# Grouped-query softmax weights scaled before their transposes, output kept feature-major

## The chip, the cores and the metric

The kernel runs on one core of one Trainium2 chip. The metric is device time in microseconds of one execution. Three timed runs of the kernel before gave a median of 2794.3 us (2793.43 to 2796.57). TensorE (PE) multiplies into the partial-sum memory PSUM, VectorE (DVE) and ScalarE (ACT) read PSUM and SBUF, GpSimd (POOL) reads SBUF, and SyncE (SP) issues the transfers.

## The reference

The whole model has two layers over 1024 tokens of width 1024. The change lies in the first layer, in the grouped-query attention, one of two head groups whose outputs go side by side into one output projection:

```python
def gqa_attention(q, k, v):
    scale = HEAD_DIM ** -0.5

    def block(qb):
        s = jnp.einsum('bqgrd,bkgd->bgrqk', qb, k).astype(jnp.float32) * scale
        pr = jax.nn.softmax(s, axis=-1).astype(v.dtype)
        return jnp.einsum('bgrqk,bkgd->bqgrd', pr, v)

    return from_blocks(lax.map(block, to_blocks(q)))
...
    a_o = rms_norm(diff_attention(a_q, a_k, a_v, lam), subln) * (1.0 - lam_init)
...
    b_o = gqa_attention(b_q, b_k, b_v)
    mix = jnp.concatenate([a_o.reshape(b, s, A_V), b_o.reshape(b, s, B_Q)], axis=-1)
    return mix @ w_out
```

There are eight query heads of 64 features and two key-value heads, so four query heads share one key-value head. After this mixer come a gated feed-forward with a convolution, a gated input embedding, a second layer with neighbourhood attention, and a final norm. All data is float32.

## The kernel before, in words

**Precision.** A float32 product is made of three fast ones: each operand is split into a high part (a copy to the type fp32r) and a low part (operand minus high part). A helper, `mm3` (lines 172 to 177), issues high by high, low by high and high by low. The high part is usually a copy on ACT, the low part a subtraction on DVE.

**Units and steps.** The function `even` computes the first mixer. It has six units: 0 to 3 are the four differential heads (A), 4 and 5 the two key-value groups of the grouped-query heads (B). A list `its` holds the steps (line 1087): eight blocks of 128 queries for each A unit, which makes steps 0 to 31, and eight blocks with four heads j = 0 to 3 for each B unit, which makes steps 32 to 95. Two B heads make a pair, an even step and the odd step after it.

**What one B step does.** `qk(n)` (line 955) computes the 128 x 1024 scores of a head into a PSUM tile S (two such tiles exist) by four matmuls, two with 128 rows (L969) and two with 64 (L974), and DVE takes the negated row maximum (L977). `exp(n)` (L986) has ACT write P = exp(S - max) to SBUF and the row sums to a small column. `combine(n)` (line 989) does, on odd steps alone, the reciprocal of both sums of a pair (L1001). `tr(n)` (line 1003) turns P on PE by eight 128 x 128 transposes (L1012) into two PSUM banks, and ACT copies the high part to `pt` (L1022); `tr2(n)` has DVE subtract for the low part (L1034). `pv(n)`, on odd steps alone, multiplies both heads of a pair by the values in sixteen matmuls of 256 columns (L1049). The stationary operand holds the high part of the values in its first 64 columns and the low part in the other 64, so output partitions 0 to 63 and 64 to 127 hold two shares of the same 64 features, and the columns are 2 x 128 queries. `tail_a(n)` adds the shares: ACT copies the upper half (L1066), DVE adds it to the lower (L1067). `tail_b(n)` turns the 64 x 256 sum back to queries by features with two PE transposes (L1078), and DVE multiplies by the reciprocals into a 256-wide tile `MS` (L1083). After four heads `place_b` hands two 128 x 128 halves of `MS` to `place` (line 1090), which transposes them again (L1095), because the output projection wants features on partitions, and splits them into H, its operand (ACT L1098, DVE L1099).

**Order.** The order is written out by hand: `step(n)` (line 1111) is a generator in two halves, and every engine runs its instructions in the order in which the program issues them. For a B step n the first half is: scores of n and their maximum; transposes of n-2 with ACT's copies; exponential of n; low parts of n-2. The second half is: `combine(n)`; on the steps where n-3 is odd, that is even n, `pv(n-3)`; `tail_b(n-4)`, which does something on odd n; `tail_a(n-3)`; and on every fourth step `place_b(n-5)`. The driver (lines 1180 to 1204) puts other work between the halves or behind them, by lists at the top of the file: a piece of the output projection's first half (`GEMM`: steps 57, 59, 61, 63, then 67, 70, 73 and so on to 100; twelve 512-column matmuls at L175 to L177 and a DVE addition at L258), the last input projection (`PROJ5`: 33, 35 and 37 among the B steps; 24 matmuls of 384 columns, then copies by ACT and DVE), transposes and splits of the next unit's queries and keys (`FIN4`: steps 28 to 32; `FIN5`: 49 to 59, odd; their DVE part, L922 or L942 to L945, comes between the halves of the step after), and the placing of the A heads (`PLACE`: 40 to 54, even; four transposes, and L1098 and L1099 of 512 columns). Weight tiles are split by `W.pump` (L164, L165) as room comes free. POOL's rotary embedding for the last unit runs in pieces in the first B steps.

**Buffers.** PSUM has four banks (`psb`) that are handed out in turn to transposes, values, tails, placing and projection; a new user waits until the one four places earlier is read out. SBUF tiles `os` come from a pool of seven, small columns from one of 24.

Of the kernel before, what the change touches and what calls it, by code (L numbers as in the profile page):

```python
# [11 lines left out]
F32 = mybir.dt.float32  # L12
F32R = mybir.dt.float32r
AF = mybir.ActivationFunctionType
ALU = mybir.AluOpType
# [10 lines left out]
P = 128  # L26
# [80 lines left out]
class Kern:  # L107
# [662 lines left out]
    def even(self, W, ready, load, after):  # L770
        nc, a = self.nc, self.a
# [25 lines left out]
        own = (slice(0, 64), slice(64, 128))  # L797
        bg = deque()

        def background(n):  # L800
            while bg and n > 0:
                bg.popleft()()
                n -= 1
# [149 lines left out]
        L, MS = {}, {}  # L953

        def qk(n):
            u, qt, j = its[n]
            A = u < 4
            if A and qt == 0:
                M[u] = self.u([P, NT, P], F32, "mix")
            qs, ks, kl = st[u]["q"], st[u]["k"], st[u]["kl"]  # L960
            e = L[n] = {"P": [], "nm": [], "S": []}
            e["s"] = self.col(2) if j % 2 == 0 else L[n - 1]["s"]
            bs = (0, 1) if A else (j,)
            qc = slice(qt * P, (qt + 1) * P)
            halves = (slice(0, 512), slice(512, 1024))
            for b in bs:
                ps = self.tS()
                for hk in halves:
                    nc.tensor.matmul(ps[:, hk], qs[b][:, qc], ks[b % 2][:, hk], start=True, stop=False)  # L969
                e["S"].append(ps)  # L970
            for hk in halves:
                for b, ps in zip(bs, e["S"]):
                    o = own[b % 2]
                    nc.tensor.matmul(ps[:, hk], qs[b][o, qc], kl[o, hk], start=False, stop=True)  # L974
            for ps in e["S"]:
                nm = self.col()
                nc.vector.tensor_reduce(nm, ps, axis=AX.X, op=ALU.max, negate=True)  # L977
                e["nm"].append(nm)

        def exp(n):  # L980
            u, qt, j = its[n]
            e = L[n]
            for b, (ps, nm) in enumerate(zip(e.pop("S"), e.pop("nm"))):
                p = self.u([P, S], F32, "P")
                c = b if u < 4 else j % 2
                nc.scalar.activation(p, ps, AF.Exp, bias=nm, accum_out=e["s"][:, c:c + 1])  # L986
                e["P"].append(p)

        def combine(n):
            u, qt, j = its[n]  # L990
            e = L[n]
            if u < 4:
                r = e["r"] = self.col(3)
                s0 = e["s"][:, 0:1]
                nc.vector.reciprocal(r[:, 0:2], e["s"])
                nc.vector.scalar_tensor_tensor(r[:, 2:3], s0, nlam, r[:, 1:2], op0=ALU.mult, op1=ALU.mult)
                nc.vector.scalar_tensor_tensor(e["P"][0], e["P"][1], r[:, 2:3], e["P"][0],
                                               op0=ALU.mult, op1=ALU.add)
            elif j % 2 == 1:
                r = e["r"] = self.col(2)  # L1000
                nc.vector.reciprocal(r, e["s"])  # L1001

        def tr(n):
            u, qt, j = its[n]
            e = L[n]
            w = e.pop("P")[0]
            e["T"] = []
            for h in range(2):
                ps = self.tb()
                for b in range(4):  # L1010
                    kt = 4 * h + b
                    nc.tensor.transpose(ps[:, b * P:(b + 1) * P], w[:, kt * P:(kt + 1) * P], self.ident)  # L1012
                e["T"].append(ps.rearrange("p (b c) -> p b c", b=4))
            if u < 4:
                e["pt"] = self.u([P, NT, P], F32, "pt")
            else:
                if j % 2 == 0:
                    e["pt"] = [[self.u([P, 4, 2, P], F32R, "pt") for _ in range(2)] for _ in range(2)]
                else:
                    e["pt"] = L[n - 1]["pt"]  # L1020
                for h in range(2):
                    nc.scalar.copy(e["pt"][h][0][:, :, j % 2], e["T"][h])  # L1022
# [13 lines left out]
        def pv(n):  # L1036
            u, qt, j = its[n]
            e = L[n]
            v = st[u]["v"]
            if u < 4:  # L1040
                o = e["o"] = self.tb()
                for kt in range(NT):
                    nc.tensor.matmul(o[:, :P], e["pt"][:, kt, :], v[:, kt, :], start=(kt == 0), stop=(kt == NT - 1))
                e.pop("pt")
            elif j % 2 == 1:
                o = e["o"] = self.tb()
                for kt in range(NT):
                    for x in range(2):
                        nc.tensor.matmul(o[:, :256], v[:, kt, :], e["pt"][kt // 4][x][:, kt % 4].rearrange("p a b -> p (a b)"),  # L1049
                                         start=(kt + x == 0), stop=(kt == NT - 1 and x == 1))  # L1050
                e.pop("pt")
                L[n - 1].pop("pt")

        def tail_a(n):
            u, qt, j = its[n]
            e = L[n]
            if u < 4:
                os = e["os"] = self.os()
                ss = self.col()
                xo = M[u][:, qt, :]  # L1060
                nc.scalar.activation(os[:, :P], e["o"][:, :P], AF.Copy, scale=e["r"][:, 0:1])
                nc.scalar.activation(xo, os[:, :P], AF.Square, accum_out=ss)
                e["rs"] = self.rstd(ss, 1.0 / P)
            elif j % 2 == 1:
                os = e["os"] = self.os()
                nc.scalar.copy(os[0:64], e["o"][64:128, :256])  # L1066
                nc.vector.tensor_add(os[0:64], e["o"][0:64, :256], os[0:64])  # L1067

        def tail_b(n):
            u, qt, j = its[n]  # L1070
            e = L[n]
            if u < 4:
                xo = M[u][:, qt, :]
                nc.vector.scalar_tensor_tensor(xo, e["os"][:, :P], e["rs"], gs, op0=ALU.mult, op1=ALU.mult)
            elif j % 2 == 1:
                ps = self.tb()
                for b in range(2):
                    nc.tensor.transpose(ps[:, b * 64:b * 64 + 64], e["os"][0:64, b * P:(b + 1) * P],  # L1078
                                        self.ident[0:64, 0:64])
                if j == 1:  # L1080
                    MS[u, qt] = self.os()
                xo = MS[u, qt][:, (j // 2) * P:(j // 2 + 1) * P].rearrange("p (h d) -> p h d", h=2)
                nc.vector.tensor_mul(xo, ps[:, :P].rearrange("p (h d) -> p h d", h=2),  # L1083
                                     e["r"][:, :, None].to_broadcast([P, 2, 64]))
            L.pop(n)

        its = [(u, qt, j) for u in range(6) for qt in range(NT) for j in range(1 if u < 4 else 4)]
        N = len(its)

        def place(src, k0, t):  # L1090

            ps = self.tb()
            n = len(src)
            for k, x in enumerate(src):
                nc.tensor.transpose(ps[:, k * P:(k + 1) * P], x, self.ident)  # L1095
            v = ps[:, :n * P].rearrange("p (k c) -> p k c", k=n)
            h, l = self.hT2(slice(k0, k0 + n), slice(t * P, (t + 1) * P))
            nc.scalar.copy(h, v)  # L1098
            nc.vector.tensor_sub(l, v, h.bitcast(F32))  # L1099
# [6 lines left out]
        def place_b(n):  # L1106
            u, qt, j = its[n]
            ms = MS.pop((u, qt))
            place([ms[:, :P], ms[:, P:]], 2 * u - 4, qt)

        def step(n):

            A = lambda m: 0 <= m < 32
            B = lambda m: 32 <= m < N
            if n < N:
                qk(n)
            if A(n - 2):
                pv(n - 2)
            if B(n - 2):
                tr(n - 2)  # L1120
            if n < N:
                exp(n)
            if B(n - 2):
                tr2(n - 2)
            if A(n - 2):
                tail_a(n - 2)
            if A(n - 4):
                tail_b(n - 4)
            yield
            if A(n - 1):  # L1130
                tr(n - 1)
                tr2(n - 1)
            if n < N:
                combine(n)
            if B(n - 3):
                pv(n - 3)
            if B(n - 4):
                tail_b(n - 4)
            if B(n - 3):
                tail_a(n - 3)  # L1140
            if B(n - 5) and its[n - 5][2] == 3:
                place_b(n - 5)
            background(4 if n < 32 else 2)
            yield
# [35 lines left out]
        for n in range(N + 6):  # L1180
# [4 lines left out]
            s = step(n)  # L1185
# [511 lines left out]
```

## Time and profile before

| | before |
|---|---|
| median of three runs | 2794.3 us |
| the profiled execution's own time | 2795.31 us |
| its span | 2793.3 us |
| granted TensorE clock, mean | 0.995 |
| ACT busy over the span | 1405.2 us (50%) |
| POOL busy over the span | 668.1 us (24%) |

The span is the time from the first to the last instruction; the execution's own time has 2 us more around it. Lines of the profile name an engine, a source line of the kernel, the operation and its tiles; "PEld" is the weight load that goes ahead of a matmul, and its start shows best when PE takes up the next piece of work. In a timeline a line gives the start, the duration, what ran and how often in a row; in square brackets stands the idle time ahead of it with what ended it. "Issue" means that nothing that the profile shows was waited for. The grouped-query steps run from about 375 to 661 us.

### The profile page before, as it was taken

How to read it: one execution, taken by the hardware profiler on the slowest of the kernel's cores; microseconds unless marked ns; L12 is line 12 of the kernel's file. 1: busy time of each engine (PE TensorE's matmuls, PEld its weight loads, DVE VectorE, ACT ScalarE, POOL GpSimd, SP SyncE). 2: the span in 40 equal slices, each digit the busy share in tenths (PEclk: the TensorE clock that was granted, in tenths of full speed). 3: DMA queues.
4: the chain of work that ended last, by engine and by line, in shares of the span. 5: the costliest groups of instructions: out<-in, count | busy, mean ns of one | idle time of the engine just before them, and what ended most of it. 6: DMA issues, size and time to landing. Idle time of an engine off the chain costs nothing. (4 is left out here: it accounts for less than half of the span.)

```text
span 2793.3 us, 37183 instructions
## 1 busy us (share of the span) xinstructions
PE 2734.1 (98%) x13776; PEld 2265.0 (81%) x13776; DVE 1920.2 (69%) x3004; ACT 1405.2 (50%) x2727; POOL 668.1 (24%) x756
## 2 busy tenths in 40 slices
PE   8999999999999999999999999999999999999998
PEld 8988877777788888888887878877878888888887
DVE  5677878775777777677635666666677777767753
ACT  4455567563444444534523666766344444453532
POOL 2222751000544444100101001000244444400000
PEclk9999999999999999999999999999999999999999
DMA  4000001101134333833211111124023343472411
GB/s 161 1 24 24 27 9 46 46 16 33 39 144 150 133 118 148 297 110 128 87 68 71 37 59 48 38 70 161 16 89 136 130 151 136 170 275 83 147 46 61
DMA packets 101700, 260.77 MB, mean 93 GB/s; under 512 B 12048, under 2 KB 18320, under 8 KB 101520
## 3 DMA queue, kind: packets, MB, share of 16 engines
q1 hardware_dynamic: 101520, 258.40, 26.1%
q8 instruction: 109, 1.79, 0.3%
q14 instruction: 71, 0.58, 0.1%
HBM read 200.16 MB, written 58.20 MB: 92 GB/s over the span
## 5 line engine op out<-in xcount | busy, mean ns | idle before, releaser
L446 PE MATMUL b<-H,op 128*128 128x512 f32 x2016 | 482.5, 391 | 9.9 <-DVE T L297 6.9
L446 PEld LDWEIGHTS b<-H,op 128*128 128x128 f32 x2016 | 379.2, 189 | 90.1 <-issue 7.5
L446 PE MATMUL S<-T,op 128*128 128x512 f32 x1512 | 364.1, 390 | 2.9 <-ACT m L464 2.7
L175 PE MATMUL b<-hi,H 128*128 128x512 f32 (+1 forms) x896 | 337.9, 377 | 1.5 <-ACT H L1297 1.5
L446 PEld LDWEIGHTS S<-T,op 128*128 128x128 f32 x1512 | 283.2, 188 | 63.3 <-ACT m L464 3.2
L176 PE MATMUL b<-lo,H 128*128 128x512 f32 (+1 forms) x896 | 329.8, 368 | 0.8 <-DVE lo L165 0.8
L177 PE MATMUL b<-hi,H 128*128 128x512 f32 (+1 forms) x896 | 330.2, 368 | 0.3 <-DVE H L1298 0.3
L182 POOL TENSOR_SCALAR col<-col 128x1 f32<-128x1 f32 (+2 forms) x100 | 29.4, 294 | 1253.3 <-ACT xs L222 1074.1
L582 PE MATMUL S<-do,do 128*128 128x512 f32 x924 | 276.7, 390 | 3.6 <-ACT do L323 2.2
L582 PE MATMUL b<-do,do 128*128 128x512 f32 x924 | 275.5, 389 | 0.0
L582 PEld LDWEIGHTS S<-do,do 128*128 128x128 f32 x924 | 172.5, 188 | 41.9 <-ACT do L323 3.0
L582 PEld LDWEIGHTS b<-do,do 128*128 128x128 f32 x924 | 173.4, 188 | 36.2
L986 ACT ACTIVATE P<-S,col 128x1024 f32<-128x1024 f32 x128 | 143.4, 1121 | 111.5 <-DVE col L977 109.0
L324 DVE TENSOR_TENSOR op<-sm,op 128x512 fp32r<-128x512 f32 x168 | 131.2, 781 | 87.8 <-ACT op L323 87.0
L175 PEld LDWEIGHTS b<-hi,H 128*128 128x128 f32 x896 | 169.4, 189 | 23.0 <-ACT H L1297 1.9
L177 PEld LDWEIGHTS b<-hi,H 128*128 128x128 f32 x896 | 169.1, 189 | 21.7 <-DVE H L1298 1.2
L176 PEld LDWEIGHTS b<-lo,H 128*128 128x128 f32 x896 | 169.6, 189 | 20.8 <-DVE lo L165 2.3
L324 DVE TENSOR_TENSOR op<-raw,op 128x512 fp32r<-128x512 f32 x126 | 161.1, 1298 | 3.8 <-ACT op L323 3.4
L977 DVE TENSOR_REDUCE col<-S 128x1 f32<-128x1024 f32 x128 | 153.1, 1217 | 10.8 <-PE S L974 9.9
L175 PE MATMUL b<-H,hi 128*128 128x512 f32 x384 | 157.3, 410 | 0.2 <-ACT H L238 0.2
L177 PE MATMUL b<-H,lo 128*128 128x512 f32 x384 | 150.1, 391 | 0.0
L176 PE MATMUL b<-H,hi 128*128 128x512 f32 x384 | 149.8, 390 | 0.2 <-DVE H L239 0.2
(199 smaller groups left out, 5275.2 us busy)
## 6 DMA issues: line engine op xcount, KB each, us to landing
raw<-in_w_up SPq DMA_DIRECT2D x88, 512.0 KB, 4.4
we<-in_w_down SPq DMA_DIRECT2D x44, 512.0 KB, 5.1
g_dram<-cv SPq DMA_DIRECT2D x44, 512.0 KB, 2.6
wt_dram<-we SPq DMA_DIRECT2D x88, 256.0 KB, 3.1
wd<-wt_dram SPq DMA_DIRECT2D x88, 256.0 KB, 2.9
wd<-in_w_down SPq DMA_DIRECT2D x66, 256.0 KB, 5.3
G<-g_dram SPq DMA_DIRECT2D x64, 256.0 KB, 5.4
raw<-in_w_inc SPq DMA_DIRECT2D x24, 512.0 KB, 3.8
```

What stands on the lines that cost most here:

```text
L175: mm(out, st[0], mv[0], start=start, stop=False)
L176: mm(out, st[0], mv[1], start=False, stop=False)
L177: mm(out, st[1], mv[0], start=False, stop=stop)
L182: self.nc.gpsimd.tensor_scalar(r, ss, inv_n, EPS, op0=ALU.mult, op1=ALU.add)
L324: nc.vector.tensor_sub(o[:, 1], src, o[:, 0].bitcast(F32))
L446: mm(out, w[:, x, k], moving(n, y, k), start=(fresh and k + x + y == 0), stop=(k == 3 and x == 1), skip_group_check=True)
L582: mm(out[t], A[:, x, t * P:(t + 1) * P], B[:, y], start=(fresh and k == 0 and x + y == 0), stop=(k == NC - 1 and x == 1), skip_group_check ...
L977: nc.vector.tensor_reduce(nm, ps, axis=AX.X, op=ALU.max, negate=True)
L986: nc.scalar.activation(p, ps, AF.Exp, bias=nm, accum_out=e["s"][:, c:c + 1])
```

## The change

The weights of each B head are now scaled by their reciprocal sum on DVE before the transposes, in SBUF and in place, in each step and for the head of the step before. The output stays with features on partitions: head 0 of a pair is added into partitions 0 to 63 of `MS`, head 1 into 64 to 127, each by one ACT copy and one DVE addition of 64 x 128. The transposes of `tail_b` with the multiplication behind them, and the transposes of `place` for B, are gone. `place_b` splits `MS` straight into H, from SBUF. `place` stays for the A heads.

```diff
@@ -996,9 +996,10 @@
-            elif j % 2 == 1:
-                r = e["r"] = self.col(2)
-                nc.vector.reciprocal(r, e["s"])
+            else:
+                r = self.col()
+                nc.vector.reciprocal(r, e["s"][:, j % 2:j % 2 + 1])
+                nc.vector.tensor_scalar(e["P"][0], e["P"][0], r, None, op0=ALU.mult)
@@ -1062,9 +1063,14 @@
             elif j % 2 == 1:
-                os = e["os"] = self.os()
-                nc.scalar.copy(os[0:64], e["o"][64:128, :256])
-                nc.vector.tensor_add(os[0:64], e["o"][0:64, :256], os[0:64])
+                if j == 1:
+                    MS[u, qt] = self.os()
+                xo = MS[u, qt][:, (j // 2) * P:(j // 2 + 1) * P]
+                os, o = self.os(), e["o"]
+                for s in range(2):
+                    nc.scalar.copy(os[own[s], :P], o[own[1 - s], s * P:(s + 1) * P])
+                for s in range(2):
+                    nc.vector.tensor_add(xo[own[s]], o[own[s], s * P:(s + 1) * P], os[own[s], :P])
@@ -1072,16 +1078,6 @@
-            elif j % 2 == 1:
-                ps = self.tb()
-                for b in range(2):
-                    nc.tensor.transpose(ps[:, b * 64:b * 64 + 64], e["os"][0:64, b * P:(b + 1) * P],
-                                        self.ident[0:64, 0:64])
-                if j == 1:
-                    MS[u, qt] = self.os()
-                xo = MS[u, qt][:, (j // 2) * P:(j // 2 + 1) * P].rearrange("p (h d) -> p h d", h=2)
-                nc.vector.tensor_mul(xo, ps[:, :P].rearrange("p (h d) -> p h d", h=2),
-                                     e["r"][:, :, None].to_broadcast([P, 2, 64]))
@@ -1106,7 +1102,10 @@
-            place([ms[:, :P], ms[:, P:]], 2 * u - 4, qt)
+            v = ms.rearrange("p (k c) -> p k c", k=2)
+            h, l = self.hT2(slice(2 * u - 4, 2 * u - 2), slice(qt * P, (qt + 1) * P))
+            nc.scalar.copy(h, v)
+            nc.vector.tensor_sub(l, v, h.bitcast(F32))
@@ -1130,8 +1129,10 @@
-            if n < N:
+            if A(n):
                 combine(n)
+            if B(n - 1):
+                combine(n - 1)
             if B(n - 3):
                 pv(n - 3)
```

## The prediction

> **What bounds the kernel now.** I read the page first, then the busy time by windows over the part that the change touches (the 64 grouped-query steps and their drain, 375 to 661 us), then the timelines of single steps.
>
> ```profile
> span 2793.3 us, 37183 instructions
> ## 1 busy us (share of the span) xinstructions
> PE 2734.1 (98%) x13776; PEld 2265.0 (81%) x13776; DVE 1920.2 (69%) x3004; ACT 1405.2 (50%) x2727; POOL 668.1 (24%) x756
> ```
> ```profile
> 375.50:661.00 285.50, 283.17 (x1715) 218.12 (x1714) 219.96 (x365) 180.62 (x343) 30.29 (x46) 1.00 0.10 33
> 406.20:443.80 37.60, 36.72 (x238) 27.69 (x237) 31.91 (x54) 28.73 (x54) 19.70 (x29) 1.00 0.01 2
> 443.83:474.64 30.81, 30.64 (x203) 23.20 (x201) 29.18 (x50) 25.26 (x50) 0.00 (x0) 1.00 0.25 86
> ```
> A window row gives its length, then busy PE, weight loads, DVE, ACT, POOL. Over the whole part PE is busy 283.17 of 285.50 us: PE sets the pace. But DVE is at 77% over it, and at 95% (29.18 of 30.81) in steps 49 to 56. The change takes work from PE and gives more to DVE, so the order of one step decides. Steps 71 (odd) and 72 (even), which carry no projection work, weight loads of PE first, then DVE:
>
> ```profile
> 540.64 0.85 PEld L1012 LDWEIGHTS b<-ident,P 128*128 128x128 f32 x8 [0.36 <-DVE os L1067]
> 541.66 0.20 PEld L1078 LDWEIGHTS b<-ident,os 64*128 64x128 f32 x2 [0.17 <-issue]
> 541.93 0.30 PEld L969 LDWEIGHTS S<-ks,qs 128*128 128x128 f32 x2
> 542.59 0.29 PEld L974 LDWEIGHTS S<-kl,qs 64*128 64x128 f32 x2 [0.36 <-issue]
> 543.25 0.86 PEld L1012 LDWEIGHTS b<-ident,P 128*128 128x128 f32 x8 [0.37 <-issue]
> 544.08 1.98 PEld L1049 LDWEIGHTS b<-pt,v 128*128 128x128 f32 x16
> 546.00 0.24 PEld L1095 LDWEIGHTS b<-ident,os 128*128 128x128 f32 x2
> 546.21 0.19 PEld L969 LDWEIGHTS S<-ks,qs 128*128 128x128 f32 x1
> ```
> ```profile
> 540.75 1.23 DVE L977 TENSOR_REDUCE col<-S 128x1 f32<-128x1024 f32 x1 [0.31 <-PE S L974]
> 541.96 1.29 DVE L1034 TENSOR_TENSOR pt<-b,pt 128x512 fp32r<-128x512 f32 x2
> 543.55 0.17 DVE L1001 RECIPROCAL col<-col 128x2 f32<-128x2 f32 x1 [0.31 <-ACT P L986]
> 543.63 0.29 DVE L1083 TENSOR_TENSOR os<-b,col 128x128 f32<-128x128 f32 x1
> 543.84 1.22 DVE L977 TENSOR_REDUCE col<-S 128x1 f32<-128x1024 f32 x1
> 544.97 1.28 DVE L1034 TENSOR_TENSOR pt<-b,pt 128x512 fp32r<-128x512 f32 x2
> ```
> PE goes from transposes to scores to transposes without waiting for data (the 0.36 before a 64-row or 128-row change is the same everywhere). On DVE an instruction starts 0.08 to 0.09 before the recorded end of the one ahead (543.55+0.17 against 543.63), so a step costs it 1.13 for the maximum and 1.20 for the two low parts.
>
> **The change, part by part.**
>
> *Removed from PE.* The two 64-row transposes (L1078): eight transposes take 544.08-543.25 = 0.83, so without them the scores of step 72 could start at 541.47 instead of 541.93: 0.46 per odd step. The two placing transposes (L1095 on os): 546.21-546.00 = 0.21 in every fourth step. In a step with projection work the first saving is larger:
>
> ```profile
> 525.33 0.20 PEld L1078 LDWEIGHTS b<-ident,os 64*128 64x128 f32 x2 [0.35 <-issue]
> 525.59 0.30 PEld L969 LDWEIGHTS S<-ks,qs 128*128 128x128 f32 x2
> 526.26 0.29 PEld L974 LDWEIGHTS S<-kl,qs 64*128 64x128 f32 x2 [0.37 <-issue]
> 526.92 0.75 PEld L1012 LDWEIGHTS b<-ident,P 128*128 128x128 f32 x7 [0.37 <-issue]
> ```
> ```profile
> 525.44 0.69 DVE L258 TENSOR_TENSOR x<-b,x 128x512 f32<-128x512 f32 x1 [1.28 <-PE b L177]
> 526.04 0.15 DVE L1001 RECIPROCAL col<-col 128x2 f32<-128x2 f32 x1
> ```
> Some 0.35 goes with the 0.26 of the transposes, of which 0.04 comes back as normal spacing: 0.57.
>
> *Added to DVE: the scaling of P (128x1024, in place), once per step.* No row shows it; these bound it:
>
> ```profile
> L788 DVE TENSOR_SCALAR gs<-gs x1: 227/227/227, 80.8 to 80.8; 128x128 f32<-128x128 f32 x1
> ```
> ```profile
> L943 DVE CAST ks<-ks x20: 420/422/991, 73.2 to 475.3; 64x512 fp32r<-64x512 f32 x20
> ```
> ```profile
> L165 DVE TENSOR_TENSOR lo<-raw,hi 128x1024 fp32r<-128x1024 f32 x60 | 73.7, 1234 | 19.4 <-ACT hi L164 18.6
> ```
> ```profile
> L997 DVE SCALAR_TENSOR_TENSOR P<-P,col,P x32: 1283/1285/1722, 91.3 to 369.6; 128x1024 f32<-128x1024 f32 x32
> ```
> ```profile
> 307.62 0.15 DVE L995 RECIPROCAL col<-col 128x2 f32<-128x2 f32 x1
> 307.81 0.22 DVE L996 SCALAR_TENSOR_TENSOR col<-col,nlam,col 128x1 f32<-128x1 f32 x1
> ```
> One input, SBUF to SBUF: 227 ns at 128 elements, 422 at 512, hence 0.51 ns per element and 0.68 us at 1024. Two inputs: 1.23 at 1024. A scalar per partition adds 0.05 (1285 against 1234). So the scaling lies between 0.68 and 1.29; it has one input, which is what the cheap rows have, and I take 0.75. Its scalar is made by the reciprocal just ahead, and such a user starts 0.19 later (307.62 to 307.81). Reciprocal and scaling end 0.94 after DVE is free, and occupy 0.86.
>
> [...]
>
> *The wait this adds.* In step n DVE runs: maximum of n, low parts of n-2, reciprocal and scaling of n-1, tail sums. PE's transposes of n-1, first after the scores of n+1, now wait for that scaling. Odd step 71: low parts start at 541.96, DVE is free at 543.17, the scaling ends at 544.11, and transposes start 0.05 later, 544.16. PE is there at 543.25-0.46 = 542.79, waits 1.37, and starts 0.91 later than now. Behind it in PE's queue wait the values matmuls and the next scores, and for these the next maximum and exponential.
>
> *The even step hides it.* There PE also runs sixteen matmuls, so from its transposes to the next ones are 0.83+1.92+1.32 = 4.07 us. DVE's maximum follows the scaling, 0.1 ahead of the transposes, and ends at +1.0. ACT's first copy comes 0.75 after the transposes start (544.00 against 543.25) and takes half of 1.08:
>
> ```profile
> 544.00 1.08 ACT L1022 CAST pt<-b 128x512 fp32r<-128x512 f32 x2 [0.48 <-PE b L1012]
> ```
> So the low parts run at about +1.3 to +2.5 and the scaling ends at +3.5, 0.5 ahead of need. The reciprocals, two additions of 128 columns (two of 0.21, by the 0.29 row, for one of 0.42) and ACT's second copy lie in this slack. If it were gone they would cost 0.1 to 0.3 a pair.
>
> *The sum, by kinds of odd step* (the split of steps is by the code's lists):
> - Ten bare ones (65, 69, 71, 75, 77, 81, 83, 87, 89, 93): 0.91, less 0.21 in every second pair, 0.80 each: **+8.0**.
> - Nine with output-projection work (57, 59, 61, 63, 67, 73, 79, 85, 91): the addition L258 lies ahead of the scaling, so it ends at 526.04+0.19+0.75 = 526.98, and transposes start at 527.03 against 526.92. +0.11 less 0.105: **0**.
> - Five pairs 39 to 48, with four placing transposes of the other heads (twice 0.21) in the even step: the pair becomes 3.52 (wait to transposes, from 540.64) +4.07+0.42 = 8.0, against 37.60/5 = 7.52: **+2.5**.
> - Four pairs 49 to 56 also carry the next unit's splits. DVE is the bound, since per pair it needs 2x1.13+2x1.20+2x0.86+2x0.21+0.17 (place)+0.60 (L1099) +2x0.61 (L922) = 8.79, against 30.81/4 = 7.70: **+4.4**.
>
> ```profile
> L922 DVE SCALAR_TENSOR_TENSOR qs<-b,qs 64x512 fp32r<-64x512 f32 x32 | 22.0, 688 | 2.4 <-ACT qs L919 1.8
> ```
> ```profile
> L1099 DVE TENSOR_TENSOR H<-b,H 128x512 fp32r<-128x512 f32 x8 | 5.5, 683 | 0.4 <-ACT H L1098 0.2
> ```
> - Three with input-projection work (33, 35, 37): as step 37 shows, 403.28+0.94+0.05 = 404.27 against 403.49, 0.78 each: **+2.3**.
>
> ```profile
> 403.28 0.16 DVE L1001 RECIPROCAL col<-col 128x2 f32<-128x2 f32 x1
> ```
> ```profile
> 403.49 0.85 PEld L1012 LDWEIGHTS b<-ident,P 128*128 128x128 f32 x8 [0.37 <-DVE col L1001]
> ```
> - POOL works 19.70 us in the second window. L943 took 422 ns in the median and up to 991: I charge the difference, 0.57, to three odd steps there: **+1.7**; the bounds are 0 and six such steps, 3.4. [...]
> - The drain from step 95: two chains of transposes wait up to 0.9 each, and the rows below lose 0.35+0.26 and 1.11+0.26: **0**.
>
> ```profile
> 653.49 0.20 PEld L1078 LDWEIGHTS b<-ident,os 64*128 64x128 f32 x2 [0.35 <-issue]
> 653.75 1.96 PEld L1049 LDWEIGHTS b<-pt,v 128*128 128x128 f32 x16
> 656.83 0.20 PEld L1078 LDWEIGHTS b<-ident,os 64*128 64x128 f32 x2 [1.11 <-DVE os L1067]
> ```
> Together +18.9 us on the profiled execution's 2795.3, which lies 1.0 above the median 2794.3: **2813 us**.
>
> **Rivals.**
> *PE stays the bound* (faster): the scaling fits where DVE is idle, and only the removed transposes count: 22x0.46+10x0.57+16x0.21 = 19.2, so 2775 us. DVE's 77% speaks for it, the order of the bare step against it: even with a scaling of no length DVE is free at 543.17 for transposes that it would have to release by 543.25 to break even. It decides if reciprocal and scaling together take under 0.1, or run ahead of the low parts.
> *Loss and saving cancel*: half of the waits are covered, for instance by PSUM banks that come free earlier with fewer takers: 2794 us. The bank waits that the steps show are short, so this has little.
> *The scaling runs at one element per cycle* (1.29): 0.54 more in each of 27 odd steps and in both scalings of four pairs, 18.9 more: 2832 us.
>
> **How the numbers follow.** Forecast 0.69, one element per cycle 0.15, cancelling 0.07, PE-bound 0.09. A measurement tells 0.2%, 5.6 us, from no change. The range: upwards the slow scaling with POOL at its upper bound, 2832+1.7 = 2834 (an even-step slack used up on top of the forecast, 32x0.3 = 9.6, stays inside); downwards POOL at 0 (1.7), the terms of the fuller steps (2.5, 4.4, 2.3) gone, and the drain keeping its 0.61+1.37: 2813-12.9 = 2800. Slower 0.84, same 0.07, faster 0.09.
>
> **What would show it.** Right: L1012 of even steps waits some 1.4 us for a scaling of 0.7 to 0.8 us; bare pairs take 7.6 instead of 6.8; steps with projection work keep their length; DVE is near 9 us per pair in 49 to 56. Wrong: no idle time ahead of L1012, or a scaling of 1.3 us, or PE back to back with a stage of some 266 us.

## The result, and the profile after

The changed kernel takes 2842.0 us in the median of four runs (2841.2 to 2844.0), the kernel before 2795.3 beside it: a ratio of 1.0172 [1.0159, 1.0185], slower by 47 us. The forecast said slower, with 2813 us in a range that ended at 2834: the direction and the kind of wait came out, the size did not. One of the six runs of the kernel with the scaling on POOL took 14928 us and stays out of its ratio.

The first lines of the page after answer to those shown of before:

```profile
span 2841.9 us, 37145 instructions
## 1 busy us (share of the span) xinstructions
PE 2732.6 (96%) x13680; PEld 2271.4 (80%) x13680; DVE 1974.1 (69%) x3100; ACT 1407.1 (50%) x2759; POOL 669.4 (24%) x756
```

PE does 96 instructions less and is busy almost as long; DVE is busy 54 us more. The share of PE falls from 98 to 96%: the 48.6 us that the span has grown are idle time of PE and time at a lower clock. The profiled execution, the slowest of the four, has a mean granted clock of 0.988, before 0.995.

To see where, I cut the grouped-query steps into groups, from the first score matmul of one step to that of another: steps 33 to 38, 39 to 48, 49 to 56, 57 to 64, 65 to 94. Windows of before (the row of 49 to 56 stands in the prediction, 30.81 us), then of after; the columns are length, busy PE, weight loads, DVE, ACT, POOL, granted clock, DMA share, GB/s:

```profile
375.52:406.21 30.69, 30.69 (x188) 26.00 (x187) 21.28 (x39) 18.07 (x38) 10.58 (x18) 1.00 0.05 18
406.21:443.83 37.62, 36.74 (x239) 27.71 (x237) 31.92 (x54) 28.75 (x54) 19.69 (x29) 1.00 0.01 2
...
474.64:513.55 38.91, 38.91 (x230) 29.70 (x229) 31.77 (x52) 24.41 (x46) 0.00 (x0) 1.00 0.25 82
513.55:643.46 129.91, 129.66 (x767) 98.22 (x765) 96.68 (x155) 76.92 (x145) 0.00 (x0) 1.00 0.04 13
```
```profile
376.55:411.85 35.30, 30.41 (x187) 25.81 (x186) 25.58 (x47) 18.37 (x39) 11.19 (x19) 1.00 0.04 15
411.85:458.76 46.91, 36.52 (x223) 28.99 (x221) 41.38 (x71) 29.02 (x60) 21.51 (x28) 0.93 0.00 1
458.76:497.50 38.74, 31.10 (x191) 25.12 (x189) 35.63 (x61) 25.87 (x52) 0.00 (x0) 0.91 0.19 69
497.50:542.78 45.28, 38.52 (x219) 30.29 (x217) 38.85 (x65) 24.97 (x50) 0.00 (x0) 0.96 0.21 70
542.78:691.56 148.78, 127.53 (x723) 99.06 (x721) 120.04 (x201) 79.25 (x162) 0.00 (x0) 0.95 0.04 11
```

The five lengths add up to 267.94 before and 315.01 after: 47.1 of the 48.6 us lie here. Every group has grown, those from 57 on too, where the forecast had put nothing for the steps with output-projection work. And the clock, 1.00 before in all five, is below 1 in four of them. Behind these figures stand nine stretches of 3.41 us each at half clock: two, two, one and four in the last four groups (one such stretch in 45.28 us gives the 0.96). A tenth lies just behind, in the drain from step 95. The kernel before has none here.

One bare pair of steps, weight loads of PE, then DVE:

```profile
575.65 0.29 PEld L974 LDWEIGHTS S<-kl,qs 64*128 64x128 f32 x2 [0.37 <-issue]
577.78 0.86 PEld L1013 LDWEIGHTS b<-ident,P 128*128 128x128 f32 x8 [1.83 <-DVE P L1002]
```
```profile
574.33 1.23 DVE L977 TENSOR_REDUCE col<-S 128x1 f32<-128x1024 f32 x1
575.58 1.29 DVE L1035 TENSOR_TENSOR pt<-b,pt 128x512 fp32r<-128x512 f32 x2
576.79 0.15 DVE L1001 RECIPROCAL col<-col 128x1 f32<-128x1 f32 x1
576.97 0.75 DVE L1002 TENSOR_SCALAR P<-P,col 128x1024 f32<-128x1024 f32 x1
```

This is the forecast's picture: maximum, low parts, reciprocal, scaling back to back on DVE, and the transposes (L1013) start 0.06 after the scaling's recorded end. They stand 1.83 behind the scores, of which 0.37 is the usual spacing: a wait of 1.46, forecast 1.37. The scaling takes 753 ns in the median, forecast 0.75. The waits of PE for the scaling over the five groups stand in one row of the list of waits (waiter, releaser, us in total, times, longest):

```profile
PE b L1013 <- DVE P L1002: 50.9, 37, 3.3
```

### The profile page after: what moved, and what is told of

Its sections match the earlier page's. It is cut to its first block, busy times and chain, and to the rows that moved or that the text cites. A ratio compares the mean times of both kernels' runs of the same rounds, so it can differ in the third digit from the quotient of the medians.

```text
span 2841.9 us, 37145 instructions
## 1 busy us (share of the span) xinstructions
PE 2732.6 (96%) x13680; PEld 2271.4 (80%) x13680; DVE 1974.1 (69%) x3100; ACT 1407.1 (50%) x2759; POOL 669.4 (24%) x756
## 5 line engine op out<-in xcount | busy, mean ns | idle before, releaser
L1013 PE MATMUL b<-ident,P 128*128 128x128 f32 x768 | 106.8, 284 | 54.8 <-DVE P L1002 53.5
L175 PE MATMUL b<-H,hi 128*128 128x512 f32 x384 | 157.2, 409 | 0.2 <-ACT H L238 0.2
L1013 PEld LDWEIGHTS b<-ident,P 128*128 128x128 f32 x768 | 88.1, 145 | 80.9 <-issue 46.0
```

Source lines behind the costliest of these rows:

```text
L175: mm(out, st[0], mv[0], start=start, stop=False)
```

## The experiments

The theory to be tested: the whole loss comes from the scaling, by where it stands in DVE's queue (behind maximum, low parts and whatever else the step puts there), since PE's transposes, and all that is queued behind them, wait for it; the idle PE then loses its clock in stretches. The rivals: the new tail (ACT copies and additions of 64 partitions, splits from SBUF) costs the time; DVE simply has too much to do, wherever the scaling stands; POOL holds the scaling back. Each figure below is a median, with its ratio to the kernel before on the same chip.

**Without the scaling.**

```diff
@@ combine, B heads (after)
-                r = self.col()
-                nc.vector.reciprocal(r, e["s"][:, j % 2:j % 2 + 1])
-                nc.vector.tensor_scalar(e["P"][0], e["P"][0], r, None, op0=ALU.mult)
```


> The changed kernel without reciprocal and scaling (the softmax weights stay undivided: this part of the computation is left out). Theory A (the whole loss comes from PE waiting for the scaling, and from what that waiting does to PE's clock): only the removed transposes are left, so 2770 to 2782 us, faster than before by 15 to 22, and no half-clock stretch in the grouped-query steps beyond the one before them. Rival B (the new tail costs by itself: two ACT copies, two DVE additions and the split from SBUF in the even step): 2800 us or more.

Measured: 2777.97 us, 0.9939 [0.9922, 0.9956]. The same groups 39 to 48 and 65 to 94, windows of this kernel:

```profile
405.84:440.63 34.79, 34.05 (x222) 26.06 (x221) 31.21 (x49) 28.49 (x58) 20.04 (x29) 1.00 0.01 2
...
508.78:630.54 121.76, 120.95 (x722) 93.85 (x721) 94.13 (x140) 79.62 (x162) 0.00 (x0) 1.00 0.04 14
```

PE is busy again for nearly the whole of each window, at full clock. So the rest of the change, the removed transposes with the new tail, gains 2794.3 x 0.0061 = 17 us (the first rival of the forecast had worked out 19.2), and reciprocal and scaling cost 1.0172 - 0.9939 = 0.0233, 65 us.

**The scaling alone, in the kernel before.**

```diff
@@ combine (before)
-            elif j % 2 == 1:
-                r = e["r"] = self.col(2)
-                nc.vector.reciprocal(r, e["s"])
+            else:
+                r = self.col()
+                nc.vector.reciprocal(r, e["s"][:, j % 2:j % 2 + 1])
+                nc.vector.tensor_scalar(e["P"][0], e["P"][0], r, None, op0=ALU.mult)
@@ tail_b: the multiplication becomes a copy
-                nc.vector.tensor_mul(xo, ps[:, :P].rearrange("p (h d) -> p h d", h=2),
-                                     e["r"][:, :, None].to_broadcast([P, 2, 64]))
+                nc.vector.tensor_copy(xo, ps[:, :P].rearrange("p (h d) -> p h d", h=2))
@@ the order of a step: as in the change
-            if n < N:
+            if A(n):
                 combine(n)
+            if B(n - 1):
+                combine(n - 1)
```


> The kernel before with the scaling alone, at the place that the change gives it; the old tail and both sets of transposes stay, its multiplication by the reciprocals is a plain copy. Theory A: the transposes of even steps are released by DVE at the same time as in the changed kernel, so the bare steps are as long, and the kept transposes cost only where PE did not wait: 2830 to 2850 us. Rival B (the tail makes a large part of the loss): 2800 to 2820 us.

Measured: 2836.86 us, 1.0154 [1.0139, 1.0169]. With the old tail and all the old transposes the loss is nearly the same: the new tail is not its cause. It also shows that the two parts do not add up: the rest of the change gains 17 us where nobody waits for the scaling, and nothing here (2836.9 without it against 2842.0 with it). This trace has four half-clock stretches from step 33 to the drain (mean granted clock 0.993), the changed kernel ten (0.988); so the old transposes may also have spared PE's clock, which no run separates.

**The scaling ahead of the low parts.**

```diff
@@ first half of a step (after)
+            if B(n - 1):
+                combine(n - 1)
             if B(n - 2):
                 tr2(n - 2)
@@ second half
-            if B(n - 1):
-                combine(n - 1)
```


> The changed kernel with one move on DVE's queue: reciprocal and scaling of the step before stand ahead of the low parts instead of behind them. Same instructions on every engine. Theory A (the place in DVE's queue makes PE wait): the scaling ends some 1.2 us earlier, the wait of 1.4 to 1.5 us in bare even steps falls under 0.4, half-clock stretches mostly go, 2785 to 2805 us. Rival C (DVE's volume of work is the limit, the order doesn't matter): 2835 to 2845 us.

Measured: 2799.29 us, 1.0022 [1.0013, 1.0031]. The instructions are the same, only their order on DVE differs, and 1.5 of the 1.72% are gone. The place in the queue is not the whole loss, though: without any scaling the kernel stood at 0.9939, so the scaling still costs 0.0083 here, of the 0.0233 in the changed kernel. A bare pair of this kernel, DVE, then the transposes that wait:

```profile
550.38 1.23 DVE L977 TENSOR_REDUCE col<-S 128x1 f32<-128x1024 f32 x1
551.63 0.17 DVE L1001 RECIPROCAL col<-col 128x1 f32<-128x1 f32 x1
551.83 0.75 DVE L1002 TENSOR_SCALAR P<-P,col 128x1024 f32<-128x1024 f32 x1
```
```profile
552.64 0.75 PEld L1013 LDWEIGHTS b<-ident,P 128*128 128x128 f32 x7 [0.65 <-DVE P L1002]
```

The scaling now stands right behind the maximum, and the idle time ahead of the transposes falls from 1.83 to 0.65 us. Its windows of 49 to 56, 57 to 64 and 65 to 94 (the profiled execution is the slowest of ten, 2804.3 us):

```profile
448.79:484.52 35.73, 30.14 (x191) 22.02 (x190) 35.01 (x62) 26.06 (x53) 0.00 (x0) 1.00 0.22 74
484.52:523.39 38.87, 37.93 (x219) 28.85 (x218) 38.06 (x65) 25.13 (x50) 0.00 (x0) 1.00 0.25 82
523.39:652.28 128.89, 122.73 (x723) 95.28 (x722) 117.91 (x202) 80.34 (x162) 0.00 (x0) 0.99 0.04 13
```

From 57 on the lengths are those of before or less. In 49 to 56 DVE is busy for 35.01 of 35.73 us: there, and in 39 to 48 (42.45 against 37.62, DVE busy for 40.73), the sheer amount of DVE work is nearly the bound in this order.

**Something for PE to do in the wait.**

```diff
@@ tr, B heads (after)
                 ps = self.tb()
+                if u >= 4 and j % 2 == 0 and h == 0 and n + 1 not in GEMM + PROJ5:
+                    for b in range(12):
+                        nc.tensor.transpose(ps[:, b % 4 * P:(b % 4 + 1) * P], self.ident, self.ident)
                 for b in range(4):
```


> The changed kernel with twelve transposes of the identity ahead of the waiting transposes of even steps, into the bank that these overwrite, in steps with no projection work ahead of them. PE waits no less for the scaling, but is busy for 1.2 us of the wait. Theory A with the clock as second term (idle PE gets half-clock stretches of 3.4 us, which lengthen the steps): the ten stretches in this stage fall to three or fewer, and 8 to 17 us are won, 2825 to 2834 us. Rival D (the stretches fall where PE would wait anyway and cost nothing): 2840 to 2850 us.

Measured: 2832.73 us, 1.0138 [1.0123, 1.0153]: more work, and less time than the changed kernel, whose interval ends above. Its windows from 39 on, to be held beside those of after (33 to 38 takes 35.31 at full clock):

```profile
411.00:457.51 46.51, 40.94 (x283) 32.40 (x282) 41.27 (x71) 29.12 (x60) 21.47 (x28) 1.00 0.01 1
457.51:494.83 37.32, 34.12 (x239) 27.24 (x237) 35.45 (x61) 25.66 (x52) 0.00 (x0) 1.00 0.21 72
494.83:540.12 45.29, 38.50 (x218) 30.05 (x217) 38.87 (x65) 24.87 (x50) 0.00 (x0) 0.96 0.21 70
540.12:682.43 142.31, 135.96 (x843) 106.75 (x842) 119.98 (x201) 79.15 (x162) 0.00 (x0) 1.00 0.04 12
```

The clock is 1.00 in four of the five groups, eight of their nine half-clock stretches are gone (and the one in the drain), and the five lengths add up to 306.74: 8.3 us less than after. So the clock term is shown here: with PE busy for part of the waits eight stretches are gone, and the eight cost some 8 us. The other 38.8 of 47.1 us are waits, and at most 1.7 (half of 3.41) for the one stretch left.

**The scaling ahead of the work between the halves**, but behind the low parts.

```diff
@@ end of the first half (after)
+            if B(n - 1):
+                combine(n - 1)
             yield
@@ second half
-            if B(n - 1):
-                combine(n - 1)
```


> The changed kernel with reciprocal and scaling still behind the low parts, but ahead of everything that is put between the two halves of a step: the projections' additions and copies, the next unit's splits and the weight splits. Theory A with its second part (the steps with projection work and splits lose because these stand ahead of the scaling): bare pairs stay as they are, steps 33 to 38 and 57 to 64 come back to the length before or under it, 2824 to 2834 us. Rival (the wait arises from the low parts alone): 2838 to 2845 us.

Measured: 2829.26 us, 1.0126 [1.0111, 1.0141]. What stands between the halves, in the changed kernel, in a step of 57 to 64, DVE, then the transposes that wait:

```profile
518.72 1.39 DVE L922 SCALAR_TENSOR_TENSOR qs<-b,qs 64x512 fp32r<-64x512 f32 x2
520.13 0.16 DVE L1001 RECIPROCAL col<-col 128x1 f32<-128x1 f32 x1
520.32 0.75 DVE L1002 TENSOR_SCALAR P<-P,col 128x1024 f32<-128x1024 f32 x1
```
```profile
521.23 0.52 PE L1013 MATMUL b<-ident,P 128*128 128x128 f32 x3 [1.04 <-DVE P L1002]
```

The next unit's splits (L922, 1.39 us) run ahead of the scaling, and PE stands idle for 1.04 ahead of the transposes of an odd step, which the forecast had let the even step hide. In the next step of this pair two weight splits stand in the queue as well, one ahead of the maximum and this one ahead of the scaling:

```profile
526.75 1.22 DVE L165 TENSOR_TENSOR lo<-raw,hi 128x1024 fp32r<-128x1024 f32 x1 [0.41 <-ACT hi L164]
```

Behind them PE idles for 2.82. With the scaling moved ahead of the work between the halves the windows of 33 to 38, 39 to 48 and 57 to 64 are:

```profile
376.20:408.07 31.87, 30.31 (x186) 25.86 (x185) 25.40 (x46) 17.90 (x39) 10.38 (x18) 1.00 0.06 17
408.07:458.43 50.36, 39.62 (x223) 32.10 (x222) 42.16 (x71) 29.70 (x60) 21.80 (x29) 0.86 0.00 1
...
497.02:536.35 39.33, 37.14 (x219) 28.85 (x218) 38.04 (x64) 24.97 (x50) 0.00 (x0) 1.00 0.24 81
```

3.4 us less in the first (35.30 after) and 5.9 in the last (45.28 after, one half-clock stretch included): what both had lost was lost to background work in DVE's queue and to the idle time that it made. 39 to 48 came out longer, 50.36 for 46.91, with four half-clock stretches for two; why is open. Bare pairs without projection work stay at 7.69 and 8.02, as in the changed kernel: there it is the low parts. Where 65 to 94 is shorter (142.50 for 148.78), it is the pairs with projection work in the odd step, 8.95 for 9.61, and two half-clock stretches less.

**The scaling on POOL.**

```diff
@@ combine (after); the reciprocal goes back to the head's own step
-                nc.vector.tensor_scalar(e["P"][0], e["P"][0], r, None, op0=ALU.mult)
+                nc.gpsimd.tensor_scalar(e["P"][0], e["P"][0], r, None, op0=ALU.mult)
@@ second half
-            if A(n):
+            if n < N:
                 combine(n)
-            if B(n - 1):
-                combine(n - 1)
```


> The changed kernel with the 128x1024 scaling on POOL, which is idle in most of the grouped-query steps; the reciprocal stays on DVE, in the head's own step. Theory A: PE waits only for the scaling, and a scaling of 2.0 to 2.6 us on POOL (its 128x512 operations take 1.0 to 1.3) has a whole step's room, so the time comes close to that without scaling: 2778 to 2788 us, faster than before. Rival: POOL is late where it also embeds the last unit (steps 39 to 45) or in the short odd steps, and PE waits again: 2795 us or more.

Measured: 2805.42 us, 1.0036 [1.0023, 1.005]: 17 us above the forecast range, and what the rival had said. Two lines of the answer for the scaling's source line, then the windows of steps 33 to 64 and 65 to 94:

```profile
L1002 POOL TENSOR_SCALAR P<-P,col x64: 2832/2847/3011, 376.7 to 660.2; 128x1024 f32<-128x1024 f32 x64
...
  PEld b L1013: 30.7, 26
```
```profile
375.83:532.76 156.93, 138.19 (x811) 110.24 (x809) 122.48 (x208) 97.80 (x197) 121.45 (x78) 0.93 0.12 41
532.76:655.59 122.83, 121.22 (x723) 93.86 (x722) 98.84 (x171) 79.85 (x162) 85.95 (x31) 1.00 0.04 14
```

POOL takes 2.85 us for what DVE does in 0.75. In 65 to 94 that does not matter: 122.83 us, close to the 121.76 without any scaling. In 33 to 64 (138.03 before, by the sum of its four windows) POOL also has the last unit's norm and embedding, is busy for 121.45 of 156.93 us, and now makes PE wait in the place of DVE; the clock of 0.93 adds to it. The miss has two likely parts: the duration was taken too short, and POOL's queue was taken for free. They were not separated.

**Without POOL's norm and embedding.** In the changed kernel the operations of `rope_b` are issued for the unit before only (`if u == 4`), so that POOL has nothing to do in steps 39 to 48.

```diff
@@ rope_b (after)
-                w["r"] = self.rstd(ss, 1.0 / 64, n)
+                if u == 4:
+                    w["r"] = self.rstd(ss, 1.0 / 64, n)
@@ its caller
-                    for fs in zip(*parts):
-                        bg.extend(fs)
+                    if u == 4:
+                        for fs in zip(*parts):
+                            bg.extend(fs)
```


> The changed kernel without POOL's norm and rotary embedding of the last unit (that part of the computation is left out), so that POOL is idle during the scalings. If POOL holds up the scaling through a shared resource, as the prediction charged with 1.7 us (bounds 0 to 3.4), 2837 to 2842 us. Rival E: POOL is behind the pairs of 10 to 11 us in steps 39 to 44, and 2832 to 2836 us.

Measured: 2838.66 us, 1.0157 [1.0142, 1.0172], which overlaps the 1.0172 [1.0159, 1.0185] of the change. The slowest scaling of after, then the same instruction in this kernel, where all sixteen in steps 33 to 48 take 0.75 to 0.76 (its lines are numbered two higher):

```profile
416.89 1.38 DVE L1002 TENSOR_SCALAR P<-P,col 128x1024 f32<-128x1024 f32 x1
```
```profile
412.64 0.75 DVE L1004 TENSOR_SCALAR P<-P,col 128x1024 f32<-128x1024 f32 x1
```

After, four of the sixteen take longer (0.97, 1.38, 0.89, 0.93: 1.2 us in all, 0.63 at most), and POOL works during all four. Two others, at 412.62 and 421.09, run beside POOL's work as well and take 0.75. In the time of the kernel the 1.2 us can't be told from nothing. Part of a gain may be hidden, though: steps 39 to 48 take 48.98 us here, at a clock of 0.86 (four half-clock stretches for two), and the two more can cost up to 3.4 (half of twice 3.41).

**POOL where it is free.** Up to a step the code of before; from that step the changed tail, with the scaling on POOL and the reciprocal in the head's own step. The border is step 56 in one kernel, 44 in the other.

```diff
@@ combine (the same condition in tail_a, tail_b and place_b)
-            else:
+            elif n >= 56:
                 r = self.col()
                 nc.vector.reciprocal(r, e["s"][:, j % 2:j % 2 + 1])
-                nc.vector.tensor_scalar(e["P"][0], e["P"][0], r, None, op0=ALU.mult)
+                nc.gpsimd.tensor_scalar(e["P"][0], e["P"][0], r, None, op0=ALU.mult)
+            elif j % 2 == 1:
+                r = e["r"] = self.col(2)
+                nc.vector.reciprocal(r, e["s"])
```


> The kernel before for heads up to step 55; from step 56 on the changed tail, with the reciprocal on DVE in the head's own step and the 128x1024 scaling on POOL (2.85 us by the run with all scalings there). By theory A nothing waits for POOL in these later steps: the steps from 56 are as short as without scaling, 0.46 to 0.57 per odd step and 0.21 per fourth step less, some 11 us in all: 2780 to 2787 us, faster than before. If POOL's 2.85 us come too late in the short steps: 2793 us or more.

> The same with the border at step 44, from where POOL has no embedding left. By theory A three more pairs are won where POOL keeps up; but DVE is nearly full in steps 45 to 56, so the reciprocal comes late and POOL's 2.85 us with it: 2778 to 2790 us, within 5 us of the border at 56.

Measured: 2786.45 us, 0.9975 [0.9966, 0.9985], with the border at 56, and 2789.69, 0.9982 [0.9973, 0.9991], at 44. Both beat the kernel before; the two intervals overlap, so which border is better stays open. The windows of 57 to 64 and 65 to 94 with the border at 56:

```profile
475.13:513.99 38.86, 37.80 (x225) 29.25 (x223) 32.66 (x56) 24.69 (x48) 22.82 (x8) 1.00 0.25 82
513.99:636.79 122.80, 121.19 (x723) 93.86 (x722) 98.89 (x171) 79.84 (x162) 85.99 (x31) 1.00 0.05 14
```

In 65 to 94 PE is the bound again (121.19 of 122.80), and the removed transposes bring what they are worth: 7.1 us against 129.91.

## Why the prediction was right in kind and wrong in size

The scaling's duration, its place behind maximum and low parts, the wait of the even step's transposes, and the order of magnitude of what the other side gains (17 us) came out as argued. The 1.29 of the slow rival is the two-input row L997 (1285 ns); against it stands 0.753, and no row shows the cycles by which that rival is named. The terms of the sum, against the windows:

| steps | forecast | after | with the filler | what was missed |
|---|---|---|---|---|
| 33 to 38 | +2.3 | +4.6 | +4.6 | background work ahead of the scaling |
| 39 to 48 | +2.5, POOL +1.7 | +9.3 | +8.9 | waits on a nearly full DVE; POOL at most a small part |
| 49 to 56 | +4.4 | +7.9 | +6.5 | waits beyond DVE's volume, and 1.4 of clock |
| 57 to 64 | 0 | +6.4 | +6.4 | background work ahead of the scaling (with one half-clock stretch in both) |
| 65 to 94 | +8.0 | +18.9 | +12.4 | 6.5 of clock, and pairs whose even step hides less |
| sum | +18.9 | +47.1 | +38.8 | |

*The clock.* The forecast had no such term; 8.3 us of its error of 28.2 are this one. It let PE idle in every pair and still counted all of PE's work at full clock. In 65 to 94 PE's waits for the scaling are 1.4 us in the mean and 3.3 at most, and there were four stretches, one of them right behind a wait of 1.83 (below).

Which of the waits a stretch followed can be read more closely. In the traces of before and after the half-clock stretches begin at whole multiples of 3.41 us from one another (after: 419.53, 429.77, 474.14, which are 3 and 13 of them apart), so the time can be cut on that grid. Two waits of after have the same 1.83 us, 546.34 to 548.17 and 565.54 to 567.37; the columns are as above:

```profile
545.83:549.24 3.41, 1.58 (x12) 1.18 (x12) 3.29 (x6) 1.61 (x4) 0.00 (x0) 1.00 0.00 0
549.24:552.66 3.42, 3.42 (x17) 3.42 (x17) 2.11 (x4) 1.90 (x5) 0.00 (x0) 0.50 0.26 75
562.90:566.31 3.41, 2.64 (x14) 1.48 (x13) 3.33 (x7) 2.54 (x5) 0.00 (x0) 1.00 0.00 0
566.31:569.73 3.42, 2.36 (x15) 2.12 (x16) 3.03 (x6) 1.74 (x5) 0.00 (x0) 1.00 0.00 0
```

The first wait lies inside one interval, PE is busy for 1.58 of it, and the next interval runs at half clock. The second is split between two intervals, and the clock stays. From 375.16 to 713.08 in this trace PE idled for 1.74 us or more in ten of the 89 full-clock intervals, and half clock followed each of the ten; in the other 79 it idled for 1.53 at most, and half clock followed none. In the trace of before, from 374.12 to 664.26, it never idled for more than 0.91 of an interval, and there is no half clock. No fixed limit can be read from this: later in the trace of after an interval with 1.38 of idle PE (1945.29 to 1948.70, PE busy for 2.03) was followed by half clock as well.

*"Nine with output-projection work ... 0".* This is the step that failed most plainly. It put only the addition L258 ahead of the scaling, as one bare timeline showed it. In 57 to 64, four of the nine, the splits of the next unit stood there too, and in the pair of step 61 the weight splits; 6.4 us were lost where nothing was forecast, 5.0 of them in that one pair (14.39 against 9.42, its half-clock stretch included); with the scaling ahead of them the group lost 0.4 (39.33 against 38.91). *"Three with input-projection work"*, +2.3, failed by the same omission: +4.6, and +1.2 once the scaling stands ahead.

*"The even step hides it."* This held where no placing stands ahead of the pair, and failed where one does. Of the ten bare pairs in 65 to 94, four begin behind no placing: the one of step 71 takes 7.69 after (6.90 before, 7.6 forecast). The others begin right behind one: that of step 89 takes 8.01 (6.67 before, 7.6 forecast). There tail and placing run just ahead of the odd step's maximum, as in the pair of step 69:

```profile
562.87 0.59 DVE L1073 TENSOR_TENSOR os<-b,os 64x128 f32<-64x128 f32 x2
563.49 0.43 DVE L1108 TENSOR_TENSOR H<-os,H 128x256 fp32r<-128x256 f32 x1
563.95 1.22 DVE L977 TENSOR_REDUCE col<-S 128x1 f32<-128x1024 f32 x1
```
```profile
567.34 0.85 PEld L1013 LDWEIGHTS b<-ident,P 128*128 128x128 f32 x8 [2.23 <-issue]
```

The maximum starts at 563.95, 0.63 after PE had taken up the transposes ahead of it (563.32), and the next ones wait 2.23 where the pair of step 71 has 1.83: 0.40 more, somewhat above the 0.1 to 0.3 a pair that the prediction named as the price of the slack being gone. In the kernel with the filler, where these steps have their full clock, the four pairs lose 0.78 each, near the 0.70 forecast, and five of the others 1.35 where 0.91 was forecast. The pair of step 77 loses 2.24 (9.58 against 7.34): there a weight split (L165, 1.23 us), too, comes ahead of the maximum, which the forecast had left out; in the changed kernel PE's longest wait, 3.3, follows it.

So the ten pairs make 12.1 for 8.0, and the projection pairs of that group the other 0.3 of the 12.4.

*39 to 56.* DVE is busy for 41.38 of 46.91 and 35.63 of 38.74 us. In 49 to 56 the forecast's 8.79 of DVE work per pair was near the 35.63 / 4 = 8.91 measured; but it made that the length, and the pairs took 38.74 / 4 = 9.69, since DVE itself still idled for 3.11 us of the group. The scaling ahead of the low parts brings them to 8.93, with 0.72 of idle DVE in the group. In 39 to 48 the same order brings 42.45, near DVE's 40.73. How the rest of 39 to 48 divides among single waits stays open.

*POOL.* The term was 1.7, with bounds 0 and 3.4, the author's estimate from one long row (L943, 991 for 422 ns); no run shows that term. What the runs showed in its place: four scalings took 1.2 us longer, all four went away with POOL's work (all sixteen at 0.75 to 0.76), and the kernel's time shows none of it outside its interval.

*The drain*, forecast 0, and all else outside the steps come to 48.6 - 47.1 = 1.5 us, the tenth half-clock stretch among it.

## What to carry to other kernels

An operation put on an engine that is not the bound cost here what its consumer waited for (a scaling of 0.75 us on DVE, waits of 1.4 in the mean on PE), and this was set by all that stood ahead of it in the queue, background work included (another order alone took the ratio from 1.0172 to 1.0022): list that per kind of step before you price the move, and put the operation first in the queue. Where an engine is nearly full, no place in its queue may be good enough: DVE was 85 and 95% busy in 39 to 48 and 49 to 56, and both groups lost some 5 us even with the scaling put first. If the bound engine begins to idle in a regular pattern, count its clock as a cost of its own: here it was 8.3 of 47.1 us.

## What the runs showed of the hardware that was not expected

PE fell to half clock for single stretches of 3.41 us, nine of them in 315 us, with no wait of PE for the scaling longer than 3.3 us and a mean of 1.4; with transposes of the identity in the waits one of the nine was left. In the traces of before and after the stretches lie on a grid of 3.41 us, and from 375 to 713 us of after half clock followed the ten intervals in which PE idled for 1.74 us or more, and none of the 79 with 1.53 or less. POOL needs 2.85 us to scale 128x1024 by a scalar per partition, 3.8 times DVE's 0.75, and DVE's scaling took up to 1.38 while POOL worked (four of six scalings beside POOL's work were long, two took 0.75).
